# Block one's feed forwards with tokens standing and weights moving, and both mixers in a new order

## The chip, the cores and the metric

The kernel runs on one core of a Trainium2 chip, alone. The metric is device microseconds (us) from start to end of one execution; several executions are timed and their median is given. The profile is of one further execution.

Engines: PE is TensorE, which multiplies a standing 128x128 operand (loaded by PEld) with a moving one; DVE is VectorE, ACT is ScalarE, POOL is GpSimd, SP is the engine whose queue issues most DMAs.

## The reference, cut to what matters

Two blocks of two layers each work on 256 tokens of 1024 features, in float32:

```python
def first_block(x, ...):
    for l in range(2):
        x = x + 0.5 * swiglu_ffn(rmsnorm(x, ffn1_norm[l]), ffn1_w_up[l], ffn1_w_down[l])
        x = x + mixer(rmsnorm(x, mix_norm[l]), ...)
        x = x + 0.5 * swiglu_ffn(rmsnorm(x, ffn2_norm[l]), ffn2_w_up[l], ffn2_w_down[l])
        x = rmsnorm(x, final_norm[l])

def swiglu_ffn(h, w_up, w_down):            # 1024 -> 2 x 2816 -> 1024
    a, b = jnp.split(h @ w_up, 2, axis=-1)
    return (jax.nn.silu(a) * b) @ w_down
```

`mixer` projects to three groups of queries, keys and values (512 columns each), to a gated convolution of width 31 and to gates. Queries and keys are normalized per head and rotated; three dilated window attentions are merged by their softmax weights; the convolution is normalized over channels; both are projected, gated, summed and projected again.

```python
def second_block(x, ...):
    for l in range(2):
        p = rmsnorm_2(x, norm1[l]) @ w_in[l]
        # p: 512 columns u, 512 q, 128 k, 128 v
        y_f = fft2(u).real @ w_f + b_f      # over tokens and columns
        y_a = windowed_gqa(rope(norm(q)), rope(norm(k)), v, sink[l])
        x = x + concat(rmsnorm_2(y_f), rmsnorm_2(y_a)) @ w_o[l]
        up = dwconv_centred(rmsnorm_2(x, norm2[l]) @ w_up[l], ...)
        x = x + (silu(gate) * val) @ w_down[l]
```

## The kernel before, in words

**Data.** x lies as eight blocks of 128 features x 256 tokens. Every float32 product is formed from halves: an operand is split into a high part (`xh`, `wh`, type fp32r) and the rest (`xl`, `wl`), and three matmuls, wl x xh, wh x xh and wh x xl, add into one PSUM bank (`mm3`, lines 335 to 337).

**Weights** come as one stream of units of 128x1024, 512 KB each. `fetch` issues their DMAs on SP into four buffers; `ahead` splits them up to three units ahead of use, the high half on ACT (L317), the low on DVE (L318); `unit` hands out the next. The order of `weight_stream` is that of use.

**Two ways to multiply.** `up_pair` and `down` let 128x128 of weights stand while 256 tokens move (256 columns): the result has features in its partitions, as x has. `token_major` (L588 to L590) lets 128 tokens of `xh`, `xl` stand while 512 columns of weights move: the result has tokens in its partitions. Block one's mixer uses the second for its gated units and for q, k and v, block two's for q and the Fourier columns.

**Order.** Each engine runs its instructions in the order in which Python writes them; semaphores join the engines. Tiles come from pools with a fixed number of buffers: four PSUM banks for `acc`, four for `aux`, seventeen SBUF tiles of 4 KB per partition (`t4`).

The stages, with their times in the profile:

- `ffn1`, layer 0 (8 to 206 us): 22 pairs of up projections of features (gate and value), then 8 results over 22 blocks of features. The scale of the norm is one number per token; a sum over features on PE and `rows` (L387, fp32 products with a diagonal) spread it over all partitions as R, and `evac_up` and `evac` multiply by it. Operands and square sums of all eight blocks of x are formed before the first matmul.
- `mixer` (206 to 506): four gated units, then q, k, v by the table QKV, with the convolution's transforms (`conv_forward`, `conv_inverse`, `norm_mean`) placed between projections by the tables `after` and `mid`. Queries and keys leave PE, pass a norm and rotation on DVE and POOL (`head_norm_rope`), and are turned by PE (`transpose_to`, L572) after the next projection. Then attention, interleaved with gates, and the projections.
- the second `ffn1` (506 to 697), with the layer's final norm folded into the following scales; then the same for layer 1 (697 to 1387).
- `mixer2` of block two, layer 0 (1387 to 1488): q, then k and v, then the Fourier columns u (split into `uh`, `ul`); the transform over columns (`f1`, L994 to L996), over the sequence (`f2`), its projection (`f3`) and the output projection (`proj`) stand between the steps of the attention, by the table `fill`.
- `ffn2` (1488 to 1681): 22 pairs of up projections with a depthwise convolution over tokens, then `down`. Layer 1: `mixer2` 1681 to 1774, `ffn2` to the end.

Of the kernel before, what the change touches and what calls it, by code (L numbers as in the profile page):

```python
# [28 lines left out]
P = 128  # L29
# [54 lines left out]
def _wide(w):  # L84
    return w.reshape(4, 2, P, 512).transpose(0, 2, 1, 3)


def weight_stream(a):
    parts = []
    for l in range(DEPTH):  # L90
        w = a["w_in"][l]
        parts += [_pairs(a["ffn1_w_up"][l], NF), _down(a["ffn1_w_down"][l])]
# [4 lines left out]
        parts += [_pairs(a["ffn2_w_up"][l], NF), _down(a["ffn2_w_down"][l])]  # L97
    for l in range(DEPTH):
        w = a["w_in_2"][l]
        parts += [_wide(w[:, 512:1024]), w[:, 1024:].reshape(2, 4, P, 256).transpose(0, 2, 1, 3), _wide(w[:, :512])]  # L100
        parts += [_half(a["w_fourier_2"][l][FORDER]), _half(a["w_o_2"][l, :512]), _half(a["w_o_2"][l, 512:])]
        parts += [_pairs(a["w_up_2"][l], NF), _down(a["w_down_2"][l])]
# [99 lines left out]
class Kernel:  # L202
# [64 lines left out]
    def make_units(self):  # L267
# [12 lines left out]
        for l in range(DEPTH):  # L280
            add("w", 44, 1024)
            add_down()
            pos["d"] = 0
            add("w", 16 + 4 * 3, 1024)
            add("d", 1, FWD)
            add("w", 4 * 6 + 16 + 4 + 8 + 8, 1024)
            add("w", 44, 1024)
            add_down()
        for l in range(DEPTH):
# [3 lines left out]
            add("d", 2, 1024)  # L293
            add("w", 2 + 8, 1024)
            add("w", 44, 1024)
            add_down()
# [60 lines left out]
    def square_sum(self, blocks, scales=None):  # L357

        nc = self.nc
        s = self.rp.tile([P, S], F32, tag="sacc", name=self.nm("sacc"))  # L360
        for b, x in enumerate(blocks):
            kw = {} if scales is None else dict(scale=scales[b])
            if b == 0:
                nc.scalar.activation(s, x, AF.Square, **kw)
            else:
                q = self.t1("sq")
                nc.scalar.activation(q, x, AF.Square, **kw)  # L367
                nc.vector.tensor_tensor(s, s, q, op=ALU.add)
        return s

# [97 lines left out]
    def ffn1(self, x, o, late, meanwhile=(), natural=False):  # L468

# [3 lines left out]
        h = self.h_slots()  # L473
        R = None

        def evac_up(n, pa, pb):
            t = self.t1("t")
            nc.vector.tensor_tensor(t, pa, R, op=ALU.mult)
            nc.scalar.activation(t, t, AF.Silu)
            f = self.t1("f")  # L480
            nc.vector.tensor_tensor(f, t, pb, op=ALU.mult)
            self.split(f, *h[n])

        got, pend = None, []
        for n in range(NF):
            pend.append((n, *self.up_pair(o)))
            if n < len(late):
                got = late[n](got)
                if n == len(late) - 1:
                    R = got  # L490
            if 0 <= n - 4 < len(meanwhile):
                meanwhile[n - 4]()
            while R is not None and len(pend) > 1:
                evac_up(*pend.pop(0))
        evac_up(*pend[0])

        def evac(ob, a):
            t = self.t1("d")
            nc.vector.scalar_tensor_tensor(t, a, 0.5, R, op0=ALU.mult, op1=ALU.mult)
            if not natural:  # L500
                nc.vector.tensor_tensor(x[ob], x[ob], t, op=ALU.add)
                return
            z = self.xp.tile([P, S], F32, tag="x", name=self.nm("xn"))
            zv = z.rearrange("p (j r) -> p r j", r=4)
# [813 lines left out]
```

## Time and profile before

| | |
|---|---|
| median of 3 runs | 1970.82 us (1970.71 to 1971.87) |
| profiled execution, its own time | 1971.52 us |
| its span (first to last instruction) | 1969.7 us |
| mean granted TensorE clock | 0.992 |
| bytes moved by DMA | 338.43 MB, 172 GB/s |

Times in the rows count from the start of the span. A busy time is the union of an engine's instructions; since matmuls overlap, the duration of one says little of how often one can be issued, and the distance between starts says that. "PEclk" is the clock granted to TensorE as a share of full speed (2.4 GHz).

### The profile page before, as it was taken

What the parts mean: (1) busy time and instruction counts of PE and PEld (TensorE: products, weight loads), DVE (VectorE), ACT (ScalarE), POOL (GpSimd) and SP (SyncE); (2) the same over time, 40 slices, a digit from 0 to 9 for tenths busy, and PEclk for the clock granted to TensorE, in tenths of its full rate; (3) what the DMA queues carried; (4) which work ended last, traced back from release to release, by engine and by line L of the source; (5) the groups of instructions that cost most, each with busy time, mean ns of one, the idle gap of its engine ahead of it and who ended that gap; (6) DMA issues with size and microseconds to landing.
All of it is one profiled execution on the core that took longest, in us unless ns stands there. A gap on an engine that the chain in (4) does not pass through costs nothing.

```text
span 1969.7 us, 36890 instructions
## 1 busy us (share of the span) xinstructions
PE 1929.9 (98%) x14640; PEld 1832.0 (93%) x14640; DVE 1417.5 (72%) x2470; ACT 1100.1 (56%) x2125; POOL 110.9 (6%) x109
## 2 busy tenths in 40 slices
PE   8999999999999999999999999999899999999999
PEld 8999878899999999998787999999789999889999
DVE  6765787877666586656877676665779985779973
ACT  5544555666544455445556665444676764666652
POOL 1000022100000010000222000000200000100000
PEclk9999999999999999999999999999989999999999
DMA  8555654435555555556544345555424555434554
GB/s 266 192 179 184 212 190 150 156 129 173 181 182 177 187 177 185 175 185 218 172 166 138 119 172 184 182 175 190 147 85 166 190 183 180 156 108 168 196 176 125
DMA packets 97260, 338.43 MB, mean 172 GB/s; under 512 B 11430, under 2 KB 14086, under 8 KB 96960
## 3 DMA queue, kind: packets, MB, share of 16 engines
q1 hardware_dynamic: 93024, 325.97, 48.7%
q0 software_dynamic: 2944, 8.11, 1.8%
q8 instruction: 114, 1.87, 0.4%
q10 hardware_dynamic: 1120, 2.00, 0.3%
q14 instruction: 58, 0.48, 0.1%
HBM read 334.99 MB, written 1.05 MB: 171 GB/s over the span
## 4 chain that ended last, share of the span: by engine, by line
PE 78%; DVE 8%; issue 6%; POOL 3%; ACT 3%; DMA 1%; POOLq 0%; DVEq 0%; ACTq 0%
PE acc L335 23%; PE acc L337 23%; PE acc L336 23%; POOL rs L548 3%; DVE wl L318 2%; PE acc L588 2%; PE acc L590 2%; PE acc L589 2%; ACT wh L317 1%; PE pt L913 1%; PE Y L821 1%; PE s L796 1%; DVE ra L554 1%; DVE rb L556 1%; ACT sq L367 1%
## 5 line engine op out<-in xcount | busy, mean ns | idle before, releaser
L318 DVE TENSOR_TENSOR wl<-raw,wh 128x1024 fp32r<-128x1024 f32 (+2 forms) x632 | 756.6, 1199 | 326.1 <-ACT wh L317 321.8
L317 ACT ACTIVATE wh<-raw 128x1024 fp32r<-128x1024 f32 (+2 forms) x632 | 653.2, 1037 | 595.2 <-PE acc L337 268.4
L335 PE MATMUL acc<-xh,wl 128*128 128x256 f32 x1760 | 503.8, 286 | 5.6 <-DVE wl L318 5.6
L336 PE MATMUL acc<-xh,wh 128*128 128x256 f32 x1760 | 499.8, 284 | 0.0
L337 PE MATMUL acc<-xl,wh 128*128 128x256 f32 x1760 | 499.3, 284 | 0.0
L335 PEld LDWEIGHTS acc<-xh,wl 128*128 128x128 f32 x1760 | 339.3, 193 | 9.3 <-DVE wl L318 6.0
L336 PEld LDWEIGHTS acc<-xh,wh 128*128 128x128 f32 x1760 | 339.4, 193 | 0.3
L337 PEld LDWEIGHTS acc<-xl,wh 128*128 128x128 f32 x1760 | 339.2, 193 | 0.0
L335 PE MATMUL acc<-hh,wl 128*128 128x256 f32 x1056 | 298.8, 283 | 0.0
L336 PE MATMUL acc<-hh,wh 128*128 128x256 f32 x1056 | 298.8, 283 | 0.0
L337 PE MATMUL acc<-hl,wh 128*128 128x256 f32 x1056 | 298.8, 283 | 0.0
L335 PEld LDWEIGHTS acc<-hh,wl 128*128 128x128 f32 x1056 | 202.8, 192 | 0.0
L336 PEld LDWEIGHTS acc<-hh,wh 128*128 128x128 f32 x1056 | 202.8, 192 | 0.0
L337 PEld LDWEIGHTS acc<-hl,wh 128*128 128x128 f32 x1056 | 202.8, 192 | 0.0
L588 PE MATMUL acc<-wl,xh 128*128 128x512 f32 x480 | 189.1, 394 | 0.8 <-DVE wl L318 0.5
L590 PE MATMUL acc<-wh,xl 128*128 128x512 f32 x480 | 187.3, 390 | 0.0
L589 PE MATMUL acc<-wh,xh 128*128 128x512 f32 x480 | 187.0, 390 | 0.0
L337 PE MATMUL acc<-xn,wh 128*128 128x256 f32 x608 | 172.7, 284 | 1.2 <-DVE xn L344 1.2
L335 PE MATMUL acc<-xn,wl 128*128 128x256 f32 x608 | 172.5, 284 | 0.0
L336 PE MATMUL acc<-xn,wh 128*128 128x256 f32 x608 | 172.0, 283 | 0.0
L337 PEld LDWEIGHTS acc<-xn,wh 128*128 128x128 f32 x608 | 116.6, 192 | 2.1 <-DVE xn L344 2.0
L335 PEld LDWEIGHTS acc<-xn,wl 128*128 128x128 f32 x608 | 116.7, 192 | 0.6 <-ACT xn L343 0.5
(276 smaller groups left out, 2926.6 us busy)
## 6 DMA issues: line engine op xcount, KB each, us to landing
raw<-wts SPq DMA_DIRECT2D x576, 512.0 KB, 3.3
raw<-wts SPq DMA_DIRECT2D x48, 384.0 KB, 3.0
brow<-b_in POOLq DMA_DIRECT2D x26, 256.0 KB, 3.9
raw<-dft SPq DMA_DIRECT2D x4, 512.0 KB, 3.5
tab<-tab ACTq DMA_DIRECT2D x1, 1024.0 KB, 7.5
out<-xn SPq DMA_DIRECT2D x8, 128.0 KB, 3.5
wraw<-conv_w POOLq DMA_DIRECT2D x6, 124.0 KB, 4.7
raw<-dft SPq DMA_DIRECT2D x2, 258.0 KB, 2.6
```

What stands on the lines that cost most here:

```text
L317: nc.scalar.activation(h[:, :n], r[:, :n], AF.Copy)
L318: nc.vector.tensor_tensor(lo[:, :n], r[:, :n], h[:, :n].bitcast(F32), op=ALU.subtract)
L335: mm(out, wl, xh, start=start, stop=False, **k)
L336: mm(out, wh, xh, start=False, stop=False, **k)
L337: mm(out, wh, xl, start=False, stop=stop, **k)
L367: nc.scalar.activation(q, x, AF.Square, **kw)
L548: nc.gpsimd.tensor_tensor(rs[:, :nh], vv[:, :nh], self.mhalf[:, :nh], op=ALU.pow)
L554: nc.vector.tensor_tensor(A3, z3, cg[:, None, :].to_broadcast([P, nh, HD]), op=ALU.mult)
L556: nc.vector.tensor_tensor(half(B[:, :nh * HD]), half(zz)[:, :, ::-1, :], sg.rearrange("p (c d) -> p c d", c=2)[:, None].to_broadcast([P, n ...
L588: mm(accs[t], xh[k][:, ts], wl[:, c], start=k == 0, stop=False)
L589: mm(accs[t], xh[k][:, ts], wh[:, c], start=False, stop=False)
L590: mm(accs[t], xl[k][:, ts], wh[:, c], start=False, stop=k == KB - 1)
```

## The change

1. All four feed forwards of block one go up by `token_major` (512 columns of weights, 256 of the gate beside 256 of the value) and down by the new `down_token`; block two's layer 0 goes down by `down_token` too. Tokens then stand in the partitions: the norm's scale is a number per partition, and `rows` is not needed. The inner features are turned by four PE transposes per 256 features (`ht`), the results by eight per half of 512 (`yt`). The turns stand between the four units of the following projection; the second half of a result is turned after the first unit of the next stage (`tail`).
2. `follow` forms the operand and the square sums of the next stage block by block, as x is updated, where all were formed after the last block.
3. Block one's mixer: the order of q, k and v; half of each group of transposes is held for two units; the convolution's steps stand elsewhere.
4. Block two's mixer: the Fourier columns come before keys and values; `f1` and the transposes stand before the attention; `f2` uses plain fp32 products with tables fetched as they are, instead of split units.

```diff
-QKV = [(0, 0), (1, 0), (2, 0), (2, 1), (0, 1), (1, 1), (0, 2), (1, 2), (2, 2)]
+QKV = [(0, 0), (2, 0), (1, 0), (0, 1), (2, 1), (1, 1), (0, 2), (1, 2), (2, 2)]
...
+    def follow(self, x, gains, scales=(None,)):
+        o, sums = ([], []), [None] * len(scales)
+        def add(b):
+            for dst, part in zip(o, self.operand(x[b:b + 1], gains[b:b + 1], b)):
+                dst += part
+            for i, sc in enumerate(scales):
+                sums[i] = self.square_add(sums[i], x[b], **({} if sc is None else dict(scale=sc[b])))
+        return o, sums, add
...
+    def down_token(self, h, scale, x, add, natural=False, first={}):
...
+        def half(hf, mid):
+            accs = [self.acc(), self.acc()]
+            def part(t, k, wh, wl):
+                ts, c = slice(t * P, (t + 1) * P), slice(k % 2 * 512, (k % 2 + 1) * 512)
+                hh, hl = h[k]
+                mm(accs[t], hh[:, ts], wl[:, c], start=k == 0, stop=False)
+                mm(accs[t], hh[:, ts], wh[:, c], start=False, stop=False)
+                mm(accs[t], hl[:, ts], wh[:, c], start=False, stop=k == NF - 1)
+            for u in range(NF // 2 - 2):
+                w = self.unit(1024)
+                for k in (2 * u, 2 * u + 1):
+                    for t in range(2):
+                        part(t, k, *w)
+                for f in mid.get(u, ()):
+                    f()
+            ws = [self.unit(1024) for _ in range(2)]
+            for t in range(2):
+                for k in range(NF - 4, NF):
+                    part(t, k, *ws[k // 2 - NF // 2 + 2])
+            return accs
...
+        def turn(hf, ys):
+            for i in range(2):
+                p = self.aux("yt")
+                for j in range(2):
+                    for t in range(2):
+                        c = slice((i * 2 + j) * P, (i * 2 + j + 1) * P)
+                        nc.tensor.transpose(p[:, j * 256 + t * P:j * 256 + (t + 1) * P], ys[t][:, c], self.ident)
+                for j in range(2):
+                    ob = hf * 4 + i * 2 + j
+                    d = p[:, j * 256:(j + 1) * 256]
...
+                        nc.vector.tensor_tensor(x[ob], x[ob], d, op=ALU.add)
+                    add(ob)
+        accs, ys = half(0, first), []
+        accs = half(1, {0: [lambda a=accs: ys.extend(copies(a))], 2: [lambda: turn(0, ys)]})
+        last = copies(accs)
+        return [lambda: turn(1, last)]
...
+        def gate(c):
+            f = st["f"] = self.t2("f")
+            for t, a in enumerate(st.pop(c)):
+                r, s = st["r"][:, t:t + 1], self.t1("t")
+                nc.scalar.activation(s, a[:, :256], AF.Silu, scale=r)
+                nc.vector.scalar_tensor_tensor(f[:, t * 256:(t + 1) * 256], a[:, 256:], r, s, op0=ALU.mult, op1=ALU.mult)
+        def turn(c):
+            p = self.aux("ht")
+            for j in range(2):
+                for t in range(2):
+                    src = st["f"][:, t * 256 + j * P:t * 256 + (j + 1) * P]
+                    nc.tensor.transpose(p[:, j * 256 + t * P:j * 256 + (t + 1) * P], src, self.ident)
+            hi, lo = (z[:, c % 2 * 2:c % 2 * 2 + 2] for z in slots[c // 2])
+            self.split(p.rearrange("p (j c) -> p j c", j=2), hi, lo)
+        for c in range(NF // 2):
+            mid = {0: tail} if c == 0 else {1: [lambda: gate(c - 1)], 3: [lambda: turn(c - 1)]}
+            if c == 1:
+                mid[0] = [norm]
...
+            st[c] = self.token_major(o, None, mid)
...
-        after = {2: conv_forward, 4: lambda: conv_inverse(0)}
-        mid = {5: [lambda: conv_inverse(1)]}
+        after = {1: conv_forward, 3: lambda: conv_inverse(0), 4: lambda: (conv_inverse(1), conv_sum()), 6: conv_mean}
...
+            self.token_major(o, evac, {1: held})
+            held = todo[1:]
+            for f in todo[:1]:
                 f()
...
+        self.token_major(o, evac_q, {0: tail, 2: [tables], 3: [start]})
+        self.token_major(o, lambda t, a: self.split(a, uh[t], ul[t], st["rc"][:, t:t + 1]), {1: [lambda: x.extend(residual())]})
...
-            wh, wl = self.unit(1024)
+            w = fw[i]
...
-                    self.mm3(out, wh[:, c], wl[:, c], Ah[:, fb, ts], Al[:, fb, ts], fb == 0 and cs == 0, fb == 3, skip=True)
+                    mm(out, w[:, c], A[:, fb, ts], start=fb == 0 and cs == 0, stop=fb == 3, skip_group_check=True)
...
+        f1(0)
+        for f in turn[:2]:
+            f()
+        f1(1)
+        for f in turn[2:]:
+            f()
```

**PE, block one's up projection.** Before, 128x128 of a weight unit's halves (`wh`, `wl`) stood in each instruction and 256 columns moved, the halves of a block of tokens (`xh`, `xl`); `acc` is the PSUM bank:

```order
L336 MATMUL acc_980<-xh_148,wh_915 128x256
L337 MATMUL acc_980<-xl_149,wh_915 128x256
L335 MATMUL acc_980<-xh_148,wl_916 128x256
L336 MATMUL acc_980<-xh_148,wh_915 128x256
L337 MATMUL acc_980<-xl_149,wh_915 128x256
```

Now, at the end of one projection of 512 columns (`ht` are turned inner features, `f` the gated products of the projection before, `ident` the identity):

```order
L674 MATMUL acc_901<-wl_923,xh_192 128x512
L675 MATMUL acc_901<-wh_922,xh_192 128x512
L676 MATMUL acc_901<-wh_922,xl_193 128x512
L583 MATMUL ht_981<-ident,f_938 128x128 x4
L674 MATMUL acc_988<-wl_948,xh_140 128x512
L675 MATMUL acc_988<-wh_947,xh_140 128x512
```

Instructions of 256 columns become half as many of 512, and four transposes stand between two projections.

**PE, from the first feed forward into block one's mixer.** Before, the last result (`hh`, `hl` are the inner features) was followed by the mixer's first projection:

```order
L335 MATMUL acc_2419<-hh_187,wl_2423 128x256
L336 MATMUL acc_2419<-hh_187,wh_2422 128x256
L337 MATMUL acc_2419<-hl_188,wh_2422 128x256
L588 MATMUL acc_2570<-wl_2453,xh_2507 128x512
L589 MATMUL acc_2570<-wh_2452,xh_2507 128x512
```

Now eight transposes of the result's second half (`y`, to `yt`) stand behind the first unit of that projection:

```order
L676 MATMUL acc_1724<-wh_1677,xl_1540 128x512
L539 MATMUL yt_1743<-ident,y_1711 128x128
L539 MATMUL yt_1743<-ident,y_1713 128x128
...
L539 MATMUL yt_1764<-ident,y_1711 128x128
L539 MATMUL yt_1764<-ident,y_1713 128x128
L674 MATMUL acc_1723<-wl_1684,xh_1552 128x512
```

The four last blocks of x, which these turns complete, are needed by the second half of the same projection.

**PE, block two's mixer, layer 0.** Before, the keys' transposes (`zk` to `tr`) and `f1` (acc from `wh` and the Fourier columns `uh`, `ul`) came right behind the projection of the Fourier columns, and the scores (`s`) right behind `f1`'s first products:

```order
L590 MATMUL acc_16242<-wh_16263,xl_15929 128x512
L572 MATMUL tr_16331<-ident,zk_16206 128x128 x2
L572 MATMUL tr_16335<-ident,zk_16225 128x128 x2
L994 MATMUL acc_16388<-wh_16293,uh_16016 128x256
L994 MATMUL acc_16434<-wh_16293,uh_16016 128x256
L995 MATMUL acc_16388<-wh_16293,ul_16017 128x256
```

Now `f1` is done when the keys are turned, and one product of `f2` (`A` with the tables `fw`) and the scores follow:

```order
L1100 MATMUL acc_13146<-wl_13008,uh_12701 128x256
L658 MATMUL tr_13160<-ident,zk_13068 128x128 x2
L1113 MATMUL acc_13199<-A_13103,fw_12825 128x129
L1113 MATMUL acc_13199<-A_13103,fw_12825 128x127
...
L658 MATMUL tr_13164<-ident,zk_13087 128x128 x2
...
L1195 MATMUL s_13168<-kT_12704,qT_12703 128x256
```

The keys' transposes stand behind `f1`, and the Fourier columns have the projection of keys and values between themselves and `f1`.

## Rows read from the trace of the kernel before

**Rows 1.** The page's busy times, engine by engine, and the view of cores.
```profile
PE 1929.9 (98%) x14640; PEld 1832.0 (93%) x14640; DVE 1417.5 (72%) x2470; ACT 1100.1 (56%) x2125; POOL 110.9 (6%) x109
...
core 0: 1969.7 us, clock 0.992
```

**Rows 2.** Busy times in stretches of the span (columns in the first line).
```profile
core 0: us, PE busy (x) PEld busy (x) DVE busy (x) ACT busy (x) POOL busy (x), PEclk, DMA share, GB/s
0.00:30.00 30.00, 23.37 (x155) 22.98 (x156) 18.41 (x29) 17.40 (x27) 8.09 (x20) 0.89 0.80 254
...
206.00:280.00 74.00, 73.86 (x336) 61.15 (x335) 56.61 (x78) 43.98 (x111) 10.40 (x10) 1.00 0.61 201
280.00:400.00 120.00, 114.33 (x667) 96.30 (x666) 101.37 (x166) 66.89 (x205) 22.66 (x15) 1.00 0.48 160
...
506.00:697.00 191.00, 191.00 (x1595) 191.00 (x1594) 116.50 (x162) 90.07 (x125) 0.72 (x1) 1.00 0.53 182
...
965.00:1090.00 125.00, 117.62 (x666) 98.43 (x665) 102.47 (x170) 68.23 (x212) 24.24 (x17) 0.97 0.47 156
...
1387.00:1440.00 53.00, 46.26 (x255) 37.45 (x255) 40.19 (x110) 33.85 (x103) 10.78 (x7) 0.94 0.35 116
1440.00:1480.00 40.00, 39.33 (x288) 34.74 (x288) 31.33 (x91) 28.06 (x70) 1.53 (x2) 0.91 0.28 93
1480.00:1530.00 50.00, 48.95 (x397) 47.77 (x397) 46.42 (x96) 34.63 (x59) 0.70 (x1) 1.00 0.51 178
...
1681.00:1715.00 34.00, 33.25 (x187) 28.14 (x187) 24.66 (x48) 21.56 (x66) 7.16 (x5) 1.00 0.50 166
1715.00:1765.00 50.00, 45.40 (x346) 38.94 (x343) 37.74 (x125) 35.06 (x93) 1.44 (x2) 0.97 0.24 84
1765.00:1815.00 50.00, 48.60 (x397) 47.69 (x396) 46.24 (x94) 34.54 (x59) 0.70 (x1) 1.00 0.50 172
```

**Rows 3.** Timeline of PE, 343.5 to 347.4 us: start, us, instruction, out<-in.
```profile
343.60 0.39 PE L589 MATMUL acc<-wh,xh 128*128 128x512 f32 x1
...
345.87 0.39 PE L590 MATMUL acc<-wh,xl 128*128 128x512 f32 x1
346.10 1.03 PE L572 MATMUL tr<-ident,z 128*128 128x128 f32 x8
...
347.20 0.39 PE L589 MATMUL acc<-wh,xh 128*128 128x512 f32 x1
```

**Rows 4.** Timeline of PE, 249.9 to 251.2 us.
```profile
250.30 0.61 PE L387 MATMUL rows<-diag,ones 128*128 128x128 f32 x4
...
250.98 0.39 PE L589 MATMUL acc<-wh,xh 128*128 128x512 f32 x1
```

**Rows 5.** Timeline of PE, 1432.5 to 1435 us, with ten instructions from first start to last.
```profile
1433.09 0.27 PE L337 MATMUL acc<-Al,wh 128*128 128x130 f32 x1
...
1434.20 0.27 PE L335 MATMUL acc<-Ah,wl 128*128 128x130 f32 x1
```

**Rows 6.** Waits of PE, 965 to 1090 us: waiter<-releaser: us in total, times, longest.
```profile
PE sum L375 <- DVE m L803: 2.5, 1, 2.5
PE tr L572 <- DVE z L560: 1.8, 2, 1.1
PE acc L715 <- DVE conv L725: 1.4, 1, 1.4
PE s L796 <- ACT pT L915: 0.7, 1, 0.7
```

**Rows 7.** Waits of PE, 1387 to 1440 us.
```profile
PE acc L995 <- DVE ul L347: 2.7, 1, 2.7
PE acc L994 <- ACT uh L346: 2.1, 1, 2.1
```

**Rows 8.** Groups by line and shape: count | busy us, mean ns | idle before.
```profile
L318 DVE TENSOR_TENSOR wl<-raw,wh 128x1024 fp32r<-128x1024 f32 x580 | 708.0, 1222 | 284.2 <-ACT wh L317 280.1
...
L913 PE MATMUL pt<-ident,e 128*128 128x128 f32 x192 | 26.8, 281 | 1.7 <-DVE e L1114 1.7
...
L347 DVE SCALAR_TENSOR_TENSOR xl<-x,vec,xh 128x256 fp32r<-128x256 f32 x40 | 19.0, 480 | 7.4 <-ACT xh L346 7.4
```

More of the change, by code (lines that the diff above doesn't have):

```diff
@@ L84, in _wide, with _ffn, _halves @@
 def _wide(w):
-    return w.reshape(4, 2, P, 512).transpose(0, 2, 1, 3)
+    return w.reshape(-1, 2, P, 512).transpose(0, 2, 1, 3)
+def _ffn(up, down):
+    n = NF * P
+    return [_wide(np.concatenate([up[:, c:c + 256], up[:, n + c:n + c + 256]], axis=1)) for c in range(0, n, 256)] + _halves(down)
+def _halves(down):
+    return [_wide(down[:, c:c + 512]) for c in (0, 512)]
 def weight_stream(a):
@@ L466, in h_slots @@
         return tiles
-    def ffn1(self, x, o, late, meanwhile=(), natural=False):
+    def down_token(self, h, scale, x, add, natural=False, first={}):
         nc = self.nc
[L473 to L504, printed above, removed]
-            for i, dst in enumerate((zv[:, :2], zv[:, :1:-1, ::-1])):
-                q = lambda w: w[:, i * P:(i + 1) * P].rearrange("p (r j) -> p r j", r=2)
-                nc.vector.tensor_tensor(dst, q(x[ob]), q(t), op=ALU.add)
-            x[ob] = z
-        self.down(h, evac)
@@ L628, in tap_transform, with mixer @@
             nc.scalar.activation(W[i][:n, hs], p[:n], AF.Copy)
-    def mixer(self, l, x, o, sacc, prep):
+    def mixer(self, l, x, o, sums, add, tail, prep):
         nc = self.nc
@@ L1225, in run @@
             nc.tensor.matmul(warm[:, :P], self.ones, self.ones, start=True, stop=True)
-        o = ([], [])
+        o, sums, add = self.follow(x, [self.v(0, "ffn1_norm", b) for b in range(KB)])
         for b in range(KB):
@@ L1229, in run @@
                 self.ahead(-2)
-            for dst, part in zip(o, self.operand(x[b:b + 1], [self.v(0, "ffn1_norm", b)], b)):
-                dst += part
-        late = (lambda _: self.square_sum(x), self.rms_cols, self.rows)
+            add(b)
         gf = [self.gains(l, "final_norm") for l in range(DEPTH)]
@@ L1243, in between, with fused_norm, normed @@
                 return self.mixer_prep(l)
-        prep2 = []
+        prep2, tail, keep, extra = [], (), {}, []
+        norm = lambda: self.rms_cols(sums[0])
+        def fused_norm():
+            v1 = self.mean_cols(sums[0], D, EPS)
+            vg = self.mean_cols(sums[1], D, 0.0)
+            keep["v1"] = v1
+            return self.combine_v(v1, vg)
+        def normed(g):
+            rf = self.rows(self.rsqrt_small(keep["v1"], 2))
+            for b in range(KB):
+                nc.vector.scalar_tensor_tensor(x[b], x[b], g[b], rf, op0=ALU.mult, op1=ALU.mult)
+            return x
@@ L1246, in run @@
         for l in range(DEPTH):
             prep = []
-            self.ffn1(x, o, late, [lambda: prep.append(between(l))]
-                      + [lambda i=i: self.tap_transform(prep[0], i) for i in range(3)])
-            o = self.operand(x, self.gains(l, "mix_norm"))
-            self.mixer(l, x, o, self.square_sum(x), prep[0])
-            o = self.operand(x, self.gains(l, "ffn2_norm"))
-            s2 = self.square_sum(x)
-            self.ffn1(x, o, (lambda _: self.rms_cols(s2), self.rows),
-                      [lambda: prep2.append(self.mixer2_prep(0))] if l else (), natural=l == 1)
@@ new lines, in run @@
+            tail = self.ffn1(x, o, norm, nxt[2], tail, [lambda: prep.append(between(l))]
+                             + [lambda i=i: self.tap_transform(prep[0], i) for i in range(3)] + extra)
+            o, sums, _ = nxt
+            nxt = self.follow(x, self.gains(l, "ffn2_norm"))
+            self.mixer(l, x, o, sums, nxt[2], tail, prep[0])
+            o, sums, _ = nxt
+            norm = lambda: self.rms_cols(sums[0])
+            nxt = self.follow(x, fused[l], (None, gf[l]))
+            tail = self.ffn1(x, o, norm, nxt[2], (), [lambda: prep2.append(self.mixer2_prep(0))] if l else (), natural=l == 1)
```

210 lines of the change are left out of this document (121 added, 89 removed).

## Prediction, before the run

> **What bounds the kernel now.** I began with the page's busy times. TensorE (PE) is busy for 1929.9 of 1969.7 us, at a mean granted clock of 0.992 [rows 1]. So 39.8 us of idle time and about 0.008 x 1969.7 = 15.8 us of half clock are all that a better order could give back. Everything else must come from issuing PE's work differently.
>
> A row's duration says nothing of that, because matmuls overlap: what counts is the distance from one start to the next. The windows by stage give it for the old form. The second feed forward of layer 0 holds 1595 PE instructions in 191.0 us without an idle moment: **0.120 us** per matmul with 256 columns moving [rows 2]. The timeline gives the form the change uses, which the mixer already has: ten matmuls with 512 columns lie between the starts at 343.60 and 345.87, so **0.227 us** each [rows 3]. Two of 256 cost 0.240, one of 512 costs 0.227, and the same products are formed.
>
> The other windows show where PE loses time: the start, the mixers' second part, block two's mixers, and the start of each of block two's feed forwards. The feed forwards between lose nothing [rows 2].
>
> **The change, part by part.** The profiled execution took 1971.52 us, 1.8 more than its span; the median of the runs is 1970.82, 0.7 us lower. I reckon against 1971.5. About 0.2% (4 us) is what a measurement of this kernel tells from no change.
>
> *Turned products.* A block one feed forward has 22 x 8 x 2 x 3 = 1056 matmuls going up and 22 x 8 x 3 = 528 going down. Four of these, and block two's first down projection (528), make 4 x 1584 + 528 = 6864 of 256 columns; 3432 of 512 replace them. 6864 x 0.120 = 823.7; 3432 x 0.227 = 779.1. **Gain 44.6 us**, all on the path, since PE has no gap there.
>
> *Transposes.* Each feed forward turns its inner features, 11 groups of four, and its result, two groups of eight; block two's down projection adds two groups of eight. That is 44 groups of four and 10 of eight. Eight transposes in a 512-column stream stand between 346.10 and the second matmul behind them at 347.20: 1.10 less one step of 0.227 is 0.87 us [rows 3]. For a group of four the nearest row is four 128-column instructions of another kind: 250.98 - 250.30 - 0.227 = 0.45 us [rows 4]. 44 x 0.45 + 10 x 0.87 = **28.5 us added**, on PE's path. From below this could not be less than 256 x 0.109 = 27.9, the step within the group of eight; from above I take the duration of one transpose, 0.281 [rows 8], which gives 71.9. I use the step, as the rows are the same operation between the same neighbours.
>
> The Trainium skill speaks against the change in two places of "TensorE: Matmul & The Clock Gate". Its section "Back-to-back issue gap" puts a warm matmul at its columns over 2.4 GHz plus 2.5 ns, so that halving the count would save only 8.6 us here; the trace has 13 ns above the columns' time in both forms (0.120 and 0.227). Its "Part 4: PE-mode transpose" gives some 275 ns for a transpose inside a kernel; the trace's duration agrees (281 ns), but the step between starts is 109 ns. By the first page the sum of these two terms would be +19.9 us instead of -16.1; I go by the rows.
>
> *Smaller PE terms.* The feed forwards no longer need the scale spread over rows: four pairs of fp32 products go, each pair the very group of [rows 4], 4 x 0.45 = 1.8 us. The sequence transform `f2` ran 24 three-pass matmuls four times and 16 narrow ones, at (1434.20 - 1433.09)/10 = 0.111 us [rows 5]: 12.4 us. It becomes 40 plain fp32 products, at 0.225 each (two to the group of [rows 4]): 9.0 us. **Gain 5.2 us.** PE's work in all: -44.6 + 28.5 - 5.2 = **-21.3 us**.
>
> *Costed at nothing: VectorE, ScalarE, DMA.* A chunk of the new up projection takes PE 48 x 0.227 + 0.45 = 11.3 us. VectorE has four splits of 1.222, two gate products near 0.480 and one 512-column split, at most twice 0.480, the same operation on half the columns: 6.8 us, 60% of it [rows 8]. So the splits, which run up to three units ahead, still cover. Were that cover gone, each chunk would pay the excess on PE. A unit of weights, 512 KB, is now wanted each 12 x 0.227 = 2.72 us, 193 GB/s; the mixer's first part already lives on 201 GB/s with PE busy 73.86 of 74 us [rows 2].
>
> *Order in block one's mixers.* The windows cost 5.7 us of idle in layer 0, and 7.4 plus 0.03 x 125 = 3.8 of clock in layer 1 [rows 2]. In layer 1 four waits make most of it: the column sum of the convolution (2.5), z's transposes (1.8), the second inverse transform (1.4), the scores (0.7) [rows 6]. The change takes the sum and the second inverse to places an entire projection behind their inputs, holds half of each transpose group back by two units (5.4 us), and puts values between q and k. I let them all go, with the clock that fell after the longest, and keep some 1.3 us per layer for the forward transform, which still wants three PSUM banks and waits for VectorE. **Gain 14 us.**
>
> *Order in block two's mixers.* In layer 0, 1387 to 1480, idle is 7.4 us and the lost clock 0.06 x 53 + 0.09 x 40 = 6.8; in layer 1, 5.4 and 1.5 [rows 2]. The two longest waits are for the halves of the Fourier columns, 2.7 and 2.1 us [rows 7], which came last and were wanted at once. They now come before keys and values, so both go. Late next: keys. Their norm, POOL step and transposes follow the last projection directly, with only `f1` and q's transposes (24 x 0.120 + 0.87 = 3.8 us) between, and the softmax chain behind them has less `f2` to hide under (1.8 us instead of 2.7 a time). The queue matters too: eight residual products (3.8 us at 0.480) now stand on VectorE ahead of a split that keys and values need. I leave 7 us of loss in layer 0 and 5 in layer 1. **Gain 9 us.** On SP two table loads of 512 KB move ahead of weights; the two units they replace were as large, and the weights run six ahead, so nothing.
>
> *Between stages.* Squares and operands now follow each block of x, and the last half of each result is turned behind the first unit of the next stage. The queue behind is: PE's second unit (2.7 us) covers four additions, operand splits and sums on VectorE; with doubled sums and two weight splits these come to about 11 us, due over 7. A wait of 0.5 us each at five places: **cost 2.5 us**. Block two's feed forwards lose 1.1 and 1.4 at their start [rows 2]; I take back 1.5 in all. The start of the kernel loses 6.6 idle and 3.3 clock; all sums now come before the second unit, but the third no longer waits behind them: **gain 2 us**. Order in all: 14 + 9 + 1.5 + 2 - 2.5 = **24 us**.
>
> Sum: 1971.5 - 21.3 - 24 = **1926 us**. If order gives nothing and the 2.5 are paid, 1953; if every loss in these windows goes (about 50 us), 1900.
>
> **The rivals.** *The waits only move* (0.10). The chains of norm, softmax and transform are as long as before, and PE's shorter stream hides less; against it, the longest waits [rows 6, 7] have a named late input that is moved by several us. Then 1971.5 - 21.3 = 1950.
>
> *The turns wait* (0.04, slower). PE takes its instructions in order, so a turn whose features aren't ready holds up all behind it. There are 44 turns, with ScalarE's silu, VectorE's product and weight splits ahead of each. For it: transposes of z waited for exactly such products, 1.8 us in two waits [rows 6]. Against: gate and turn stand two units (5.4 us) apart, and VectorE has 40% free. It decides from 45/44 = 1.0 us per turn; at 1.6 us, between the waits of rows 6, 44 x 1.6 = 70 us, so 1996.
>
> *Transposes at their full duration, or halving that saves little* (0.03, no change). If PE could not overlap transposes with 512-column neighbours, 256 x (0.281 - 0.109) = 44 us come back: 1970. A fixed cost per matmul that is small would give back 36: 1962. The rows speak against both.
>
> That the change doesn't do what it says is excluded by the order of its instructions: the 512-column rows and the turns stand there.
>
> **How the numbers follow.** The forecast has 0.83, in 1908 to 1944, since its order terms may be off by two thirds either way. The first rival lies around 1950. Range: 1907 to 1950, leaving out half of the first rival, the others and the forecast's edges. Faster by over 0.2%: 0.93 (forecast and first rival); within: 0.03; slower: 0.04.
>
> **What would show it.** Feed forwards in block one near 186.5 us instead of 191, with 0.227 between 512-column starts and PE never idle; 0.45 per turn; no wait for the column sum or for Fourier halves; PE idle time near 25 us and clock above 0.995; VectorE some 60 us less busy. Wrong would be a step other than 0.227 there, waits of PE for `f` at the turns, or new waits for keys and the softmax beyond 12 us.

## The result and the profile after

The changed kernel takes 1940.68 us (median of 4 runs, 1937.02 to 1942.18) where the kernel before takes 1971.18: a ratio of 0.9842, 95% interval 0.9825 to 0.9859. That is faster by 30.5 us where 45 were forecast. A second set of runs gave 1938.22 against 1971.63, ratio 0.9824 (0.981 to 0.9839). The profiled execution is the first set's fastest, 1937.02 us.

Page and cores view of the kernel after:

```profile
PE 1900.9 (98%) x11416; PEld 1666.6 (86%) x11416; DVE 1356.4 (70%) x2280; ACT 1102.6 (57%) x2083; POOL 114.5 (6%) x109
...
core 0: 1935.2 us, clock 0.998
```

Against [rows 1], PE is busy 29.0 us less and idle 34.3 us instead of 39.8, where the prediction named 25. The page also shows 61 us less of VectorE, as said. Busy time at half clock counts full, so a part of the 29.0 is clock: by the granted clock, before lost 15.4 us to half clock within its work, this execution 3.4.

Busy times in stretches of the kernel after, columns as in [rows 2]:

```profile
0.00:30.00 30.00, 22.05 (x75) 17.69 (x76) 14.56 (x25) 15.53 (x26) 8.20 (x18) 0.89 0.75 240
...
280.00:400.00 120.00, 116.84 (x698) 99.56 (x696) 100.53 (x171) 74.03 (x244) 26.17 (x15) 1.00 0.49 161
503.70:689.90 186.20, 186.20 (x852) 154.25 (x851) 103.46 (x118) 92.41 (x117) 0.69 (x1) 1.00 0.54 186
...
955.00:1090.00 135.00, 131.43 (x825) 113.00 (x824) 112.38 (x202) 80.86 (x258) 27.43 (x17) 1.00 0.48 155
1365.50:1420.00 54.50, 49.27 (x306) 41.52 (x305) 45.55 (x130) 37.87 (x117) 7.63 (x7) 1.00 0.37 122
...
1450.00:1500.00 50.00, 47.37 (x372) 45.06 (x371) 43.75 (x90) 32.86 (x56) 0.70 (x1) 1.00 0.46 157
...
1730.00:1780.00 50.00, 47.34 (x373) 45.20 (x372) 43.92 (x90) 33.01 (x57) 0.70 (x1) 1.00 0.46 155
```

A whole feed forward now takes 186.2 us instead of 191.0, without an idle moment, as before. The kernel's start idles 8.0 us instead of 6.6, the starts of block two's feed forwards 2.6 and 2.7 instead of 1.1 and 1.4: these got worse. The first mixer's middle stretch still idles 3.2 of 120 us.

Timeline of PE in the kernel after, a group of four turns between two products:

```profile
39.21 0.39 PE L676 MATMUL acc<-wh,xl 128*128 128x512 f32 x1
39.44 0.60 PE L583 MATMUL ht<-ident,f 128*128 128x128 f32 x4
39.79 0.47 PE L674 MATMUL acc<-wl,xh 128*128 128x512 f32 x1
40.11 0.39 PE L675 MATMUL acc<-wh,xh 128*128 128x512 f32 x1
```

40.11 - 39.44 - 0.227 = 0.44 us: the 0.45 of the prediction.

Waits of PE over the whole kernel after, longest in total first:

```profile
PE acc L674 <- DVE wl L329: 4.2, 2, 2.8
PE s L888 <- ACT qkv L659: 3.8, 2, 1.9
PE tr L658 <- DVE zk L651: 3.0, 3, 1.5
PE sumc L427 <- DVE sacc L377: 2.7, 1, 2.7
PE acc L346 <- ACT xh L357: 2.4, 4, 0.8
PE acc L346 <- ACT yfh L354: 2.3, 1, 2.3
PE acc L674 <- DVE z L859: 2.2, 2, 1.1
PE acc L777 <- DVE qkv L856: 1.6, 2, 1.4
PE rows L414 <- DVE diag L413: 1.6, 4, 0.6
```

The waits of [rows 6] for the column sum, the second inverse transform and z, and those of [rows 7] for the Fourier halves, are gone. In their place stand the scores' wait for the last keys (3.8), the keys of block two (3.0), the sums at the kernel's start (2.7), and operands (xh, 2.4).

By stage, from the start of its first product to that of the next stage's, with the part lost to half clock in brackets (us; the last row ends with the start of PE's last product; `turn_clean`, `mixers_only` and `four` are experiments below):

| stage | before | after | turn_clean | mixers_only | four |
|---|---|---|---|---|---|
| ffn1, layer 0, with the start | 206.2 (3.4) | 205.1 (3.4) | 200.6 (1.7) | 210.9 (3.4) | 200.8 (1.7) |
| mixer, layer 0 | 299.6 (0) | 298.8 (0) | 300.5 (0) | 298.0 (1.7) | 299.9 (1.7) |
| second feed forward | 190.9 | 186.2 | 186.2 | 190.9 | 186.2 |
| ffn1, layer 1 | 195.2 | 189.5 | 189.5 | 193.2 | 189.4 |
| mixer, layer 1 | 304.0 (3.4) | 299.9 (0) | 306.0 (3.4) | 297.9 (0) | 298.7 (0) |
| second feed forward | 191.0 | 186.2 | 186.2 | 191.0 | 186.2 |
| block two, layer 0 | 294.0 (6.8) | 284.2 (0) | 292.4 (5.1) | 286.6 (1.7) | 284.5 (1.7) |
| block two, layer 1 | 285.4 (1.7) | 281.7 (0) | 285.5 (1.7) | 280.9 (0) | 279.8 (0) |

The brackets go by the recorded clock. At the kernel's start they are too low, for the record of the kernel after begins 12.9 us into its span: the twelve products before that stand 0.43 apart instead of 0.227, as under the half clock recorded from 16.3 us on, and so lose 2.4 us more (an estimate, 12 x 0.2).

One correction to the description ahead: instructions do not everywhere stand in the order of Python's lines. In the kernel after, products of block two's output projection (`mix`) stand between those of the following feed forward (`xh`):

```profile
1453.23 0.28 PE L347 MATMUL acc<-xh,wh 128*128 128x256 f32 x1
1453.35 0.28 PE L346 MATMUL acc<-mix,wl 128*128 128x256 f32 x1
```

The trace of the kernel before has the same mixture (1484 to 1489 us); so the framework moves instructions, and an edit can shift more than its own lines. Nor are all operands and square sums formed before the first matmul in the kernel before: its first product starts at 7.79 us, its first square at 16.34.

### The profile page after: what moved, and what is told of

Read it like the earlier page. It is cut to its first block, busy times and chain, and to the rows that moved or that the text cites. A ratio compares the mean times of both kernels' runs of the same rounds, so it can differ in the third digit from the quotient of the medians.

```text
span 1935.2 us, 30166 instructions
## 1 busy us (share of the span) xinstructions
PE 1900.9 (98%) x11416; PEld 1666.6 (86%) x11416; DVE 1356.4 (70%) x2280; ACT 1102.6 (57%) x2083; POOL 114.5 (6%) x109
## 4 chain that ended last, share of the span: by engine, by line
PE 82%; issue 8%; DVE 6%; POOL 2%; ACT 2%; DMA 1%; POOLq 0%; ACTq 0%; DVEq 0%
PE acc L674 10%; PE acc L676 10%; PE acc L675 10%; PE acc L346 10%; PE acc L348 9%; PE acc L347 9%; PE acc L507 5%; PE acc L509 5%; PE acc L508 5%; POOL rs L634 2%; DVE wl L329 1%; PE pt L1009 1%; PE ht L583 1%; PE s L888 1%; PE Y L913 1%
## 5 line engine op out<-in xcount | busy, mean ns | idle before, releaser
L329 DVE TENSOR_TENSOR wl<-raw,wh 128x1024 fp32r<-128x1024 f32 (+1 forms) x618 | 749.2, 1216 | 405.9 <-ACT wh L328 405.3
L328 ACT ACTIVATE wh<-raw 128x1024 fp32r<-128x1024 f32 (+1 forms) x618 | 647.7, 1052 | 574.0 <-PE acc L676 264.6
L674 PE MATMUL acc<-wl,xh 128*128 128x512 f32 x1184 | 470.7, 398 | 6.7 <-DVE wl L329 4.2
L676 PE MATMUL acc<-wh,xl 128*128 128x512 f32 x1184 | 463.6, 392 | 0.0
L675 PE MATMUL acc<-wh,xh 128*128 128x512 f32 x1184 | 462.7, 391 | 0.0
L674 PEld LDWEIGHTS acc<-wl,xh 128*128 128x128 f32 x1184 | 223.5, 189 | 54.4 <-DVE wl L329 5.0
L675 PEld LDWEIGHTS acc<-wh,xh 128*128 128x128 f32 x1184 | 223.7, 189 | 44.5
L346 PE MATMUL acc<-xh,wl 128*128 128x256 f32 x352 | 103.4, 295 | 2.6 <-ACT xh L357 2.4
L348 PE MATMUL acc<-xl,wh 128*128 128x256 f32 x352 | 99.1, 285 | 0.4 <-DVE xl L358 0.4
L347 PE MATMUL acc<-xh,wh 128*128 128x256 f32 x352 | 98.9, 282 | 0.0
```

The costliest lines, as they stand in the source:

```text
L328: nc.scalar.activation(h[:, :n], r[:, :n], AF.Copy)
L329: nc.vector.tensor_tensor(lo[:, :n], r[:, :n], h[:, :n].bitcast(F32), op=ALU.subtract)
L346: mm(out, wl, xh, start=start, stop=False, **k)
L347: mm(out, wh, xh, start=False, stop=False, **k)
L348: mm(out, wh, xl, start=False, stop=stop, **k)
L674: mm(accs[t], xh[k][:, ts], wl[:, c], start=k == 0, stop=False)
```

## The experiments

**The turn apart from the mixers.** `turn_only` puts both mixers back and leaves the feed forwards as changed; `mixers_only` does the reverse.

```diff
-QKV = [(0, 0), (2, 0), (1, 0), (0, 1), (2, 1), (1, 1), (0, 2), (1, 2), (2, 2)]
+QKV = [(0, 0), (1, 0), (2, 0), (2, 1), (0, 1), (1, 1), (0, 2), (1, 2), (2, 2)]
...
-            self.token_major(o, evac, {1: held})
+            self.token_major(o, evac, {1: mid.get(j, ())})
...
-        self.token_major(o, lambda t, a: self.split(a, uh[t], ul[t], st["rc"][:, t:t + 1]), {1: [lambda: x.extend(residual())]})
...
-            w = fw[i]
+            wh, wl = self.unit(1024)
```

> Both mixers back in the order of the kernel before (its table of q, k, v, its places for the convolution's steps, all transposes behind the next projection; in block two q, keys and values, Fourier columns, the split units for the sequence transform); the feed forwards as changed. Theory A: 1971 less 16.1 for products and transposes and 1.8 for the scales' rows, with 2 either way for the starts of stages: 1951 to 1956 us. Theory B: the turn gives little, 1963 to 1970 us. A mixer of block one in it should take about 299.6 us plus 0.9 for the turned result, as before.

> Block one's four feed forwards and block two's first down projection back to weights standing and 256 columns moving, with the scale spread over rows; operands and square sums still follow x block by block; both mixers as changed. Theory A: 1971 less 3.4 for the sequence transform and 10 to 17 for waits and clock: 1951 to 1958 us. Theory B: less the forecast's 24 and 3.4: 1942 to 1946 us.

`turn_only`: 1959.9 us (ratio 0.9939, 0.9924 to 0.9954), between the two theories: 11.7 us gained. `mixers_only`: 1955.14 (0.9914, 0.9899 to 0.9929), in theory A's span. In both, each layer's second feed forward takes what the table has for its form, 186.2 or 190.9 to 191.0. The missing part of `turn_only` must lie elsewhere: its first stage takes 205.3, as the changed kernel's does, and its profile lost 3.4 us more to half clock than that of before (18.8 against 15.4). And `mixers_only`, with the old first feed forward, needs 210.9 for it instead of 206.2. What both share is the sums formed block by block (`follow`), at the start.

**The turns themselves.** Each transpose of the feed forwards is issued a second time.

```diff
                     nc.tensor.transpose(p[:, j * 256 + t * P:j * 256 + (t + 1) * P], src, self.ident)
+                    nc.tensor.transpose(p[:, j * 256 + t * P:j * 256 + (t + 1) * P], src, self.ident)
```

> Every transpose of the feed forwards is issued twice into the same place: 256 more of them. Theory A (each stands on PE's path at its step of 0.109 us): 256 x 0.109 = 27.9 us more than the changed kernel in the same call, 26 to 30. Rival (a transpose's full duration counts, 0.28): 65 to 72 us more. Rival (they slip between 512-column products at no cost): under 8 us more.

1971.0 us against 1938.22 for the changed kernel in the same set (`after_again`, below): 32.8 more, 2.8 beyond theory A's span. Its page of cores has the clock at 0.993 instead of 0.998, so some of it is half clock. A second feed forward, which has none, takes 191.8 instead of 186.2; its 52 further transposes at 0.109 make 5.7. Timeline of PE, one doubled group:

```profile
50.70 0.28 PE L584 MATMUL ht<-ident,f 128*128 128x128 f32 x1
50.82 0.27 PE L585 MATMUL ht<-ident,f 128*128 128x128 f32 x1
...
51.47 0.27 PE L585 MATMUL ht<-ident,f 128*128 128x128 f32 x1
...
51.81 0.39 PE L677 MATMUL acc<-wh,xh 128*128 128x512 f32 x1
```

51.81 - 50.70 - 0.227 = 0.88, twice 0.44, although each row lasts 0.27. Both rivals fall: transposes are neither hidden nor paid at their duration, and theory A's step holds where no half clock blurs it.

**The clock.** 

> The changed kernel once more, nothing edited. Theory A (the turned products and their transposes cost what was predicted; what is missing lies in the order terms, some of it in half clock that comes in some executions and not in others): 1937 to 1942 us, and a profile with a second stretch at half clock beside that of the kernel's start if its mean granted clock is near 0.994, at a place where PE waited before. Theory B (the forecast's order terms came in full, the turn of the products gave less): the same time, but idle time of PE and half clock together near 24 us below those of the kernel before.

1934.56 to 1939.04 us, median 1938.22. PE idles 32.4 us in the profile and loses 3.4 to half clock, 35.8 against 55.2 before: 19.4 less, where theory B wanted 24. Theory A's condition, a profile near 0.994, did not come: the profile has the clock at 0.998 and a stretch of 3.4 us at half clock from 372 us on, 2 us behind the end of the scores' wait of 1.9. Over both sets, three executions at 0.998 took 1934.6 to 1937.9, five at 0.994 or 0.995 took 1938.6 to 1942.2. Where the further stretches lay in these wasn't profiled.

**The start.** The squares come after the first unit's products, the first norm one unit later.

```diff
-        o, sums, add = self.follow(x, [self.v(0, "ffn1_norm", b) for b in range(KB)])
+        o, sums = ([], []), []
...
-            add(b)
+            for dst, part in zip(o, self.operand(x[b:b + 1], [self.v(0, "ffn1_norm", b)], b)):
+                dst += part
...
+            if c == 1 and slow:
+                mid = {1: [norm], 2: [lambda: gate(c - 1)], 3: [lambda: turn(c - 1)]}
...
-        prep2, tail, keep, extra = [], (), {}, []
+        prep2, tail, keep, extra = [], [lambda: sums.append(self.square_sum(x))], {}, []
```

> The changed kernel, but at its start the square sums are formed after the first unit's products, as before the change, and the first norm, gate and turn stand one unit of weights later. Theory A (at the start, the sums between the operand splits hold up the split of the second unit of weights and PE's sums, 2.7 and 1.4 us of waiting at half clock): 3 to 5 us less than the changed kernel (1938 to 1941), so 1934 to 1937 us, and the first mixer begins near 201.5 us instead of 203.4 to 205.0. Rival (the start is bound by the loads of x and weights, as before): within 1 us of the changed kernel.

1932.59 us, ratio 0.9802 (0.9789 to 0.9816), 1.4 us below theory A's span. The first mixer begins at 200.5. ScalarE's timeline in the changed kernel:

```profile
13.63 0.51 ACT L357 ACTIVATE xh<-x,vec 128x256 fp32r<-128x256 f32 x1 [1.38 <-DMA x<-x]
14.05 0.40 ACT L376 ACTIVATE sq<-x 128x256 f32<-128x256 f32 x1
14.35 0.49 ACT L357 ACTIVATE xh<-x,vec 128x256 fp32r<-128x256 f32 x1
14.75 0.40 ACT L376 ACTIVATE sq<-x 128x256 f32<-128x256 f32 x1
15.06 1.04 ACT L328 ACTIVATE wh<-raw 128x1024 fp32r<-128x1024 f32 x1
```

and with this edit:

```profile
11.46 1.04 ACT L328 ACTIVATE wh<-raw 128x1024 fp32r<-128x1024 f32 x1
12.52 0.51 ACT L357 ACTIVATE xh<-x,vec 128x256 fp32r<-128x256 f32 x1
14.31 0.51 ACT L357 ACTIVATE xh<-x,vec 128x256 fp32r<-128x256 f32 x1 [1.29 <-DMA x<-x]
```

In the kernel before, the same split stood ahead of the last two blocks of x:

```profile
12.47 1.04 ACT L317 ACTIVATE wh<-raw 128x1024 fp32r<-128x1024 f32 x1
13.42 1.12 ACT L346 ACTIVATE xh<-x,vec 128x256 fp32r<-128x256 f32 x2
```

And PE's second unit, in the changed kernel and with this edit:

```profile
17.78 0.79 PE L674 MATMUL acc<-wl,xh 128*128 128x512 f32 x1 [1.40 <-DVE wl L329]
```

```profile
13.81 0.50 PE L676 MATMUL acc<-wl,xh 128*128 128x512 f32 x1 [1.50 <-DVE wl L329]
```

The second weight split began at 15.06, behind the last square; now at 11.46, between loads of x. The squares' own time is the small part: from 13.63 on, the two that stand ahead of the split take 0.3 us each from start to next start, 0.6 of the 2.6 us that it began later than in the kernel before. The rest is its place in ScalarE's queue, behind the last two blocks of x, for which ScalarE idled 1.38. Why the framework put it there isn't shown, nor what part of the gain comes from the norm, which this edit moves too.

**Sums ahead of block two's feed forwards.**

```diff
-            nxt = self.follow(x, self.gains(l, "norm2_2"))
-            self.mixer2(l, o, stats1 if l else stats, (lambda: x) if l else lambda: normed(gf[1]), nxt[2], tail, prep2[l])
-            o, sums, _ = nxt
+            self.mixer2(l, o, stats1 if l else stats, (lambda: x) if l else lambda: normed(gf[1]), lambda b: None, tail, prep2[l])
+            o = self.operand(x, self.gains(l, "norm2_2"))
+            sums = [self.square_sum(x)]
```

> The changed kernel, but ahead of block two's two feed forwards the operand and the square sums are formed after the last block of x, as before the change. Theory A (ScalarE's squares between the splits of the operand delay the first up projections: waits for xh of 1.2 us and some for the scale in both layers, where the kernel before idled 1.1 and 1.4): 2 to 3 us less than the changed kernel, 1935 to 1938 us. Rival (the waits come from the last block of x itself and remain, with the operand still later): the same time, or up to 2 us more.

1934.06 us (0.9808, 0.9792 to 0.9824), below theory A's span, with an interval that overlaps the changed kernel's. The wait for xh of 1.2 us at 1450 to 1500 is replaced by one of 0.7 for the last sums of the mixer (as). Without half clock, block two's layers take 282.3 and 280.7 instead of 284.2 and 281.7: 2.9 us. Its executions lie at 1930.7 and 1931.0 (clock 0.996, 0.997) and at 1937.1 twice (0.993, 0.994). So theory A has the size about right. Its reason, the squares on ScalarE, is not what the changed kernel's trace shows. VectorE, ScalarE and PE in it:

```profile
1450.85 1.22 DVE L329 TENSOR_TENSOR wl<-raw,wh 128x1024 fp32r<-128x1024 f32 x1
1452.00 0.42 DVE L1164 TENSOR_TENSOR xn<-xn,as 128x256 f32<-128x256 f32 x1
```

```profile
1452.45 0.51 ACT L357 ACTIVATE xh<-xn,vec 128x256 fp32r<-128x256 f32 x1 [1.63 <-DVE xn L1164]
```

```profile
1453.01 0.39 PE L346 MATMUL acc<-xh,wl 128*128 128x256 f32 x1 [0.70 <-ACT xh L357]
```

PE waits for xh, but ScalarE had idled 1.63 us for the block of x (`xn`), which VectorE formed behind a weight split. The edit moves operand and squares together: it shows that following x block by block costs 2.9 us here, and not which instruction's place is to blame.

**The last keys.**

```diff
-            self.token_major(o, evac, {1: held})
+            last = j == len(QKV) - 1
+            self.token_major(o, evac, {1: held, 2: todo[:1] if last else []})
...
-            for f in todo[:1]:
+            for f in [] if last else todo[:1]:
```

> The changed kernel, but in block one's mixers the first half of the last keys is turned inside the last projection, behind its third unit, instead of right ahead of the scores. Theory A (the scores wait 1.9 us in each layer for the copy of just these transposes, which stands behind a weight split on ScalarE): 3 to 4 us less than the changed kernel, and no wait of the scores for the copy. Rival (the softmax behind the scores is late next, so the wait moves to its transposes): within 1 us of the changed kernel, with a new wait of about 1.9 us some microseconds later.

1938.67 us (0.9828, 0.9815 to 0.9842): no measurable gain. ScalarE and PE in the changed kernel show why the wait was there, the copy behind a weight split:

```profile
370.36 1.04 ACT L328 ACTIVATE wh<-raw 128x1024 fp32r<-128x1024 f32 x1
371.31 0.58 ACT L659 ACTIVATE qkv<-tr 128x512 f32<-128x512 f32 x1
```

```profile
368.59 0.60 PE L658 MATMUL tr<-ident,z 128*128 128x128 f32 x4
...
371.94 0.38 PE L888 MATMUL s<-qkv,qkv 64*128 64x128 f32 x2 [1.90 <-ACT qkv L659]
```

With the turn a unit earlier that wait is gone: the first scores start at 367.98 with no idle moment ahead of them. A wait of 1.5 stands some 10 us behind them instead, in the second group of scores, for the copy of the other half of these keys, which has the softmax's exponentials (`e`) ahead of it on ScalarE (ScalarE, then PE, in this run):

```profile
376.50 0.71 ACT L900 ACTIVATE e<-e,m 128x512 f32<-128x512 f32 x1
377.21 0.57 ACT L659 ACTIVATE qkv<-tr 128x512 f32<-128x512 f32 x1
```

```profile
377.84 0.49 PE L889 MATMUL s<-qkv,qkv 64*128 64x128 f32 x4 [1.48 <-ACT qkv L659]
```

Layer 1 shows the same, 1.47 us at 1052.20 instead of 1.89 at 1047.51. So the rival holds in the main: the wait went behind the softmax, and is 1.5 us there instead of 1.9.

**The residual products of block two.** In the changed kernel ScalarE waits 5.5 us for a load between 1360 and 1420:

```profile
ACT wh L328 <- DMA raw<-wts: 6.2, 2, 5.5
```

```diff
-        self.token_major(o, lambda t, a: self.split(a, uh[t], ul[t], st["rc"][:, t:t + 1]), {1: [lambda: x.extend(residual())]})
+        self.token_major(o, lambda t, a: self.split(a, uh[t], ul[t], st["rc"][:, t:t + 1]), {})
...
-        fill = {0: [lambda: f2(0)], 1: [lambda: f2(1)], 2: [lambda: (f3(0), f3(1)), lambda: (f3(2), f3(3))],
+        fill = {0: [lambda: f2(0)], 1: [lambda: f2(1)], 2: [lambda: (f3(0), f3(1)), lambda: (f3(2), f3(3)), lambda: x.extend(residual())],
```

> The changed kernel, but in block two's first mixer the eight products that scale x for the residual stand behind the attention's third step instead of inside the projection of the Fourier columns. Theory A (on VectorE's queue they hold up weight splits; these free the buffers that SP's loads wait for, so ScalarE's next weight split waits 5.5 us for its load and the copy of the keys stands behind it; PE pays 0.9 for a weight split and about 2 for the keys): the wait of 0.9 and most of the keys' waits in layer 0 go, 2 to 3 us less than the changed kernel at equal clock, and ScalarE's wait for a load falls under 2 us. Rival (the products collide with the softmax where they now stand): the same time or up to 2 us more, with new waits of PE for e or yfh in that mixer.

1937.76 us (0.9822, 0.9808 to 0.9835). ScalarE's wait for a load falls to 1.6, PE's for the weight split is gone, and block two's layer 0 takes 285.4 us, 1.1 more. PE's waits in that mixer:

```profile
PE tr L658 <- DVE zk L651: 1.7, 1, 1.7
PE pt L1009 <- DVE e L1218: 1.2, 1, 1.2
PE acc L346 <- ACT yF L1126: 1.1, 1, 1.1
```

So the chain through the load was real, but PE still waits for the keys; the rival holds, with the softmax (e) late as well. On VectorE of this run the norm of the second keys (`vv`) stands behind a weight split:

```profile
1398.92 1.22 DVE L329 TENSOR_TENSOR wl<-raw,wh 128x1024 fp32r<-128x1024 f32 x1
1400.05 0.22 DVE L632 TENSOR_SCALAR vv<-ss,evc 128x2 f32<-128x2 f32 x1
```

**Edits together.** `all_three` joins start, late sums and keys; `four` adds the residual products; `two` has start and late sums alone.

> The three edits together (start, sums ahead of block two's feed forwards, last keys). Theory A: the gains add up, 8 to 12 us less than the changed kernel, 1927 to 1932 us, which is the predicted time less what clock and remaining waits cost. Rival: 1936 to 1940 us, the waits have only moved.

> All four edits together (start, sums ahead of block two's feed forwards, last keys, residual products). Theory A: the waits removed are gone from PE's path and, with fewer of them close together, the half clock in block two's mixers comes in fewer executions: 1926 to 1931 us, and executions within 5 us of each other. Rival: 1932 to 1936 us as with three of them, spread over some 10 us by the clock.

> The changed kernel with the start's edit and the late sums alone, the last keys and the residual products as changed. Theory A (these two carry the gain; the keys' wait shrank by 0.4 and the residual's move gave nothing): 1929 to 1933 us, as the four together, at equal clock within 1.5 us of them. Rival (the other two edits matter): 1934 to 1937 us.

| | median us | ratio to before | executions |
|---|---|---|---|
| all_three | 1933.46 | 0.9803 (0.9785 to 0.9821) | 1927.9 to 1937.6 |
| four | 1930.34 | 0.9782 (0.9769 to 0.9795) | 1928.7 to 1930.8 |
| two | 1931.21 | 0.9794 (0.9779 to 0.9808) | 1930.6 to 1935.7 |

`all_three` lies between its theory and its rival, and its interval overlaps the changed kernel's. `four` is within theory A, its executions 2.1 us apart; it is the fastest measured and lies 42 us below before. `two` already has what `four` has, within the intervals: theory A. The intervals of `two` and `four` lie clear of the changed kernel's.

**The turn alone.** Old mixers with start and late sums, the edits as above.

> Both mixers in the order of before, and the square sums where they were before at the kernel's start and ahead of block two's feed forwards: what is left of the change is the turned products with their transposes. Theory A (the turn is worth what was predicted, and the run with the old mixers fell short by what the block by block sums cost, 4 at the start and 3 in block two): 1971.5 less 16.1 and 1.8, within 2: 1952 to 1956 us; a first mixer that begins near 201 us. Rival (the turn itself is worth only the 11.7 that the run with the old mixers showed): 1958 to 1961 us.

1953.66 us against 1972.54, ratio 0.9905 (0.9889 to 0.9922): 18.9 us, where 17.9 was worked out. Theory A holds, within what the clock blurs (its executions have 0.989 to 0.994, those of before in the same set 0.990 to 0.996). Sums and operands still follow x at block one's other stages in it. What leaves no such doubt is the second feed forwards, without idle time and half clock: 186.2 instead of 190.9 and 191.0.

## Why the prediction was right, and where it was not

The measured time lies in the range, the direction is right, and the size is two thirds of the forecast (30.5 of 45.3 us), so 14.7 us are missing. (The forecast's 1908 to 1944 is a little wider than it says: two thirds of the 24 would be 1910 to 1942.) Point by point:

- **Turned products and transposes, -16.1, with the scales' rows -17.9: right.** `turn_clean` shows 18.9, the feed forwards stand at 186.2, a group of four at 0.44, and `f2`'s fp32 products cost 0.22 each, as priced. Against the rules of the Trainium skill's "TensorE: Matmul & The Clock Gate" the trace holds: by the gap of its section "Back-to-back issue gap", which it gives for a single matmul by itself, these terms would have come to a loss of 19.9. The duration that its "Part 4: PE-mode transpose" gives agrees with the rows (0.27) and was not what a transpose cost (0.109).
- **Between stages, and the start: the step that failed.** "all sums now come before the second unit" was booked as a gain of 2; beside the turn's 4.7 us the first stage gained only 1.1, so the start lost 3.6: more idle time, and half clock for longer. The weight split that PE's second unit needs stood on ScalarE behind the last blocks of x and their squares. The starts of block two's feed forwards were booked as a gain of 1.5 and lost 2.9, there with PE waiting for operands whose blocks of x were late on VectorE. That is 10 of the 14.7 us; `two`, which undoes just that, is at 1931.21, 7.0 us below the changed kernel's second set and 9.5 below its first. At block one's other stages no wait came, so the cost of 2.5 was too much. Nor did the forecast see that PE had idled 1.1 us at the start of layer 1's first feed forward (697 to 735 us); the prediction has it that the feed forwards between lose nothing. That went as well.
- **Block one's mixers, 14: about half.** The waits named did go, but the scores' for the last keys and one for a PSUM bank (z, 1.1 a layer) came in their place: idle and half clock fell by 1.4 us in layer 0 and 5.4 in layer 1 (over each mixer's windows), and 3.4 of the 5.4 is half clock that this execution didn't have. This is the rival that the waits only move, in part; `keys_early` shows one of them moving.
- **Block two's mixers, 9: more than that in the profiled execution** (idle and half clock from 14.2 to 5.5 us in layer 0 and from 7.0 to 2.2 in layer 1), though the keys were late next as said. But 8.5 of these 13.5 us is half clock that this execution was spared; idle time alone fell by 5.
- **Clock.** The sum took the clock as won. It was in the profiled execution, at 0.998; the other three of its set have 0.994 or 0.995, and the median lies 3.7 us above it. Which stages lost it there no profile shows.
- The turns' rival fell: PE never waited for f, nor had it an idle moment in a feed forward that follows a mixer.

Together, 10 us at the starts, 14 - 6.8 = 7.2 in block one's mixers and 3.7 of clock came out short, and 13.5 - 9 = 4.5, 2.5 and 1.1 came out better than forecast: 12.8 of the 14.7. That the time lies so well within the range owes something to errors of opposite sign: the turn was worked out, while the order terms came near by luck in part.

## What to carry to other kernels

Price a matmul by the distance between starts, and a transpose between matmuls likewise; then a reshaping of a dense stretch can be reckoned within what a measurement tells (17.9 against 18.9 us here). When work is moved earlier "as inputs come", look at which queue it enters: there it can stand ahead of whatever the critical engine waits for next, and here one weight split behind the last blocks of x and their squares cost 3.6 us, more than the first mixer's new order gained (1.4). A short instruction can cost far more than its duration when it changes the place of the next. Removing a stage's longest waits returned about half of them in block one's mixers, since the next chain was not far behind: discount such gains, and look for a wait that went away some microseconds further on.

## What was not expected of the hardware

The same program's executions differ by up to 10 us, about what the clock alone would make: `all_three` took 1927.9 us at a mean granted clock of 0.999 and 1937.6 at 0.994, and 0.005 x 1930 is 9.7. And more PE work did not come with more clock: `turns_twice` keeps PE busier in its feed forwards, and yet its ten executions have 0.991 to 0.996, the changed kernel's eight 0.994 to 0.998. Its profile has stretches at half clock of 3.4 to 6.8 us at four places in mixers where the changed kernel's first profile has none; one profile of each doesn't show that these places are typical.
